# A decoder trunk on one core: split weights kept in DRAM, the place ahead of the MLP reordered, and the convolution tied behind the wide block's queries

## The chip, the cores and the metric

The kernel runs on one core of a Trainium2 chip. The metric is the device time of one execution in microseconds; a kernel's time is the median of several runs. TensorE (PE) does the matrix products, VectorE (DVE) and ScalarE (ACT) the elementwise work, GpSimd (POOL) a little of it, and SyncE (SP) issues nearly all DMAs.

## The reference

One layer over 1024 rows of width 1024, all in float32. `mix` stands for the recurrent parts in the middle:

```python
h = rms_norm(x, norm_mix)
xa, ga, q, f, v, g, m_a, m_b = split(h @ w_in)          # eight projections of 1024
xa = causal_depthwise_conv(xa, conv_w, conv_b)          # four taps
y_a = rg_lru(xa, w_r, w_i, lam) * gelu(ga)              # gated linear recurrence
o = hgrn2_chunkwise(silu(q), (1-lb)*sigmoid(-f), log(f_gate), v)
y_b = rms_norm(o, hg_norm) * silu(g)
x = x + (sigmoid(m_a) * y_a + sigmoid(m_b) * y_b) @ w_out
h = rms_norm(x, norm_mlp)
x = x + square(relu(h @ w_up)) @ w_down
return rms_norm(x, norm_final)
```

## The kernel before, in words

**Products.** Every float32 product is made of three matmuls (`mm3`, L130): each operand is split into a high part, rounded to the fast float32 form by ScalarE (`split`, L87), and the rest, which VectorE subtracts (L88); then high x high, high x low and low x high are summed in PSUM. A weight tile of 128 x 1024 is thus loaded raw (`load_w`, L95, 512 KB), cast on ScalarE and subtracted on VectorE before PE can use it.

**Stages in time.** The mixer works on two halves of 512 rows (c = 0, 1) and four pairs of heads (p), which makes eight stages i = 4c + p. Stage i+1's projections on PE are interleaved with the recurrent block `hgrn` of stage i: `go(n)` in `hgrn` runs n steps of the next stage. The weights of a pair are used twice, once in each half, and are loaded and split both times. After the mixer come the gate products (16 "quads", seven products each by a Strassen-like plan, `PLAN`), the output projection, the second norm with its transposes, the MLP's up products (16 quads, the same plan) and the down products.

**Weight order.** `seq` lists the weight tiles in the order of use: 72 projection tiles (36 different ones), four tiles of gate weights used at the end of the mixer, then three rounds of eight output tiles: one for rows 0 to 511 (`out_proj`), and one for each of the two "parts" (256 rows each) of the second half. `next_w` hands out the next tile, and `fill_w` loads and splits ahead of it. Raw tiles have four buffers, split tiles six (three pairs of high and low).

**Order of work.** A planner puts every engine's instructions in order by priority (place in the program, raised by `high_priority`) and by its own estimate of when each is ready; each engine, SP's queue of DMAs too, then works strictly in that order. Where `pinned` is set PE keeps the order of the program. It is set in the mixer from the end of stage 0's first projection on.

**Around the change.** In `hgrn`, three blocks of small products are made per stage (L513), then VectorE works out `kc`, `qb`, `kk` and last `qf` (L598 to L612, the helper's line is L503), and PE multiplies `qf` by `kk` in the wide block (L642). `pk` (L668) transposes `kk` after one more multiply on VectorE. The next stage's convolution (`conv`, L405, three passes on each of two tiles, L411) is emitted during the q projection; its split result `xcH`, `xcL` is read by the products `pr` and `pi` of `rg_lru`. In the second half GpSimd also makes operand combinations for the gates (`make_combos`, L303).

Ahead of the MLP the residual rows go out to `x2d` (L871), come back as `x2a` (L1150), are normed (`norm_rows`, L151), transposed on PE (L1161) and split into the operands B11, B21, B22, B12. From these `combos` makes t1, n2, T3, T4 (L893 to L896). The rows of the second half come straight from the output projection's second half (L1190). `quad_steps` turns the raw tiles of a quad into its weights: "a" is A11, "sums" and then "b" and "c" give s1 to s4, "d" gives A12 and A22.

Of the kernel before, what the change touches and what calls it, by code (L numbers as in the profile page):

```python
# [44 lines left out]
def trunk(ctx: ExitStack, tc: tile.TileContext, x, wts, mlp, pv, gains, mask_f, mask_u, out):  # L45
# [28 lines left out]
    for c in range(NC + 1):  # L74
        seq += [wts[MIX_TILES + j] for j in range(OUT_TILES)]
    most = [n_mix]
    ready, made = {}, [0]
# [11 lines left out]

    def raw_tile(name):  # L90
        return wp.tile([P, 1024], F32, tag="raw", name=name, bufs=4)
# [5 lines left out]

    def split_w(i, raw):
        h = wp.tile([P, 1024], F32R, tag="w", name=f"wH{i}", bufs=6)
        lo = wp.tile([P, 1024], F32R, tag="w", name=f"wL{i}", bufs=6)  # L100
        with tc.high_priority(400):
            split(raw, h, lo)
        return h, lo
# [3 lines left out]
    def fill_w(n):  # L107
        while made[0] < min(n, most[0]):
            i = made[0]
            raw = raws.pop(0) if raws else load_w(i)  # L110
            ready[made[0]] = split_w(i, raw)
            made[0] += 1

    def get_w(i, ahead=2):
        fill_w(i + ahead + 1)
        return ready.pop(i)
# [288 lines left out]
    def conv(c, p, xc, xps):  # L405
        for s in range(2):
# [3 lines left out]
            for j in range(3):  # L410
                V.scalar_tensor_tensor(  # L411
# [6 lines left out]
                )  # L418
            if c + 1 < NC:
                G.tensor_copy(xcar[:, u, :], xp[:, T : T + 3])  # L420
# [78 lines left out]
    def hgrn(c, p, got, go):  # L499
# [112 lines left out]
        mul(pairs(qf)[:, :, 1, :], q8[:, :, 1, :], t8[:, :, 0:1].to_broadcast([P, 16, 32]))  # L612
# [146 lines left out]
    def stage(i):  # L759
# [19 lines left out]
        def convolve():  # L779
            got["xc"] = conv(c, p, xc, xps)  # L780
# [124 lines left out]
    def quad_steps(i, pools, raws=raw_tile, minus=False):  # L905
# [22 lines left out]
        def pair(src, names):  # L928
            def go():
                h, lo = (pools[1].tile([P, 1024], F32R, tag="w", name=f"w{names[0]}{i}{q}", bufs=6) for q in "HL")  # L930
# [128 lines left out]
    def ykt(c, ku):  # L1059
        p, s = divmod(ku, 2)  # L1060
        t = yt[c][p]
        s = s if c == 0 else 1 - s
        return t[:, 0, s, :], t[:, 1, s, :]

# [7 lines left out]
    for q in own[:2]:  # L1072
        load_quad(GQ + q, dma=in_turn if q == own[0] else load_late)
        gwork[q] = quad_steps(GQ + q, (w1p, wp), minus=True)
        with tc.high_priority(600):
            gwork[q]["a"]()
            if q == own[0]:
                gwork[q]["sums"]()
                gwork[q]["d"]()
    for o in ("t1", "n2"):  # L1080
        load_combo(o)
    in_turn(raw_q[GQ + own[1]][1], mlp[GQ + own[1], 1])
    for o in ("T3", "T4"):
        load_combo(o)
# [4 lines left out]
    gwork[own[0]]["b"]()  # L1089
# [4 lines left out]
    for q in own:  # L1094
# [3 lines left out]
        for step in (1, 2, 4, 5, 6) if q == own[0] else (0, 1, 2, 3, 4, 5, 6):  # L1098
# [4 lines left out]
            if q == own[0] and step == 2:  # L1103
# [14 lines left out]
            for k in {2: ("sums", "a", "b"), 5: ("c",), 6: ("d",)}.get(step, ()):  # L1118
                if q > own[0] or k != "a":
                    gwork[n][k]()  # L1120
        gate_work(q)
# [3 lines left out]
    close_hB()  # L1125
    y1p, close_y = opened("y1p")
    y_tiles(y1p, 1)
# [7 lines left out]
    n2p, close_n2 = opened("n2")  # L1135
# [329 lines left out]
```

## Time and profile before

| | |
|---|---|
| median of 3 runs | 1588.41 us (1586.48 to 1588.73) |
| profiled execution, its own time | 1585.07 us |
| its span, first to last instruction | 1583.3 us |
| busy: PE / DVE / ACT / POOL | 1531.4 / 1209.5 / 820.8 / 162.6 us |
| granted clock of TensorE, mean | 0.992 |
| DMA moved | 280.07 MB, mean 177 GB/s |

The span in 40 equal slices, each digit the busy share in tenths:

```profile
PE   7989999999999999999999978999999999999998
...
DVE  5797586696876938686856488988778888888877
ACT  5656756557475534454533376777677632211113
POOL 1021110234436600000000000000000000000000
```

A slice is 39.6 us. The mixer ends in the fifteenth, the gates run to the middle of the twenty-third, the place ahead of the MLP is the twenty-fourth and twenty-fifth (PE 7 and 8), up products follow to the thirty-second and the down products to the end. In the views a row of the timeline is: start, duration, engine, line, operation, output <- inputs, shapes, count, and in brackets the idle time before it with what ended it. A row of the windows view is: window, its length, then busy time and (x) instructions for PE, PE's weight loads, DVE, ACT and POOL, then the granted clock, the DMA share and GB/s.

### The profile page before, as it was taken

To read this page: it belongs to the slowest core of one execution; us is meant where nothing else is said; L and a number is where in the kernel's file an instruction comes from. 1 tells how busy PE (TensorE), PEld (TensorE's weight loads), DVE (VectorE), ACT (ScalarE), POOL (GpSimd) and SP (SyncE) were. 2 spreads that over 40 slices of the span, in tenths; PEclk is the share of its full clock that TensorE was granted. 3 is DMA by queue.
4 is the path that set the end of the run, shared out by engine and by line. 5 is a ranking of instruction groups with operands and counts; after the bars stand their busy time and mean duration, and the time that the engine had idled before them with its cause. 6 is when DMAs were issued, how large, how long until landed. Compare 5 with 4: busy or idle time off the path is not lost.

```text
span 1583.3 us, 23131 instructions
## 1 busy us (share of the span) xinstructions
PE 1531.4 (97%) x9072; PEld 1278.8 (81%) x9072; DVE 1209.5 (76%) x1706; ACT 820.8 (52%) x1341; POOL 162.6 (10%) x187
## 2 busy tenths in 40 slices
PE   7989999999999999999999978999999999999998
PEld 6878888888788888888888767888888878888886
DVE  5797586696876938686856488988778888888877
ACT  5656756557475534454533376777677632211113
POOL 1021110234436600000000000000000000000000
PEclk9999999999999999999999999999999999999999
DMA  6223122232343375332328762766666675666652
GB/s 241 96 94 107 67 103 85 94 121 94 134 137 118 106 269 199 130 117 96 134 95 310 260 212 80 279 253 252 253 249 248 226 273 226 246 255 254 254 199 107
DMA packets 72205, 280.07 MB, mean 177 GB/s; under 512 B 7712, under 2 KB 16032, under 8 KB 59168
## 3 DMA queue, kind: packets, MB, share of 16 engines
q1 hardware_dynamic: 69072, 267.58, 45.3%
q10 hardware_dynamic: 3024, 11.01, 1.9%
q8 instruction: 71, 1.16, 0.3%
q14 instruction: 38, 0.31, 0.1%
HBM read 193.63 MB, written 84.93 MB: 176 GB/s over the span
## 4 chain that ended last, share of the span: by engine, by line
PE 76%; DVE 13%; ACT 6%; issue 2%; DMA 2%; POOL 1%; DVEq 0%; SPq 0%; POOLq 0%; ACTq 0%
PE dX L132 3%; PE dX L133 3%; PE uX L132 3%; PE dX L134 3%; PE uX L134 3%; PE gX L134 3%; PE gX L133 3%; PE uX L133 3%; PE gX L132 3%; PE uY L134 2%; PE gY L134 2%; PE gY L133 2%; PE uY L132 2%; PE uY L133 2%; PE gY L132 2%
## 5 line engine op out<-in xcount | busy, mean ns | idle before, releaser
L88 DVE TENSOR_TENSOR wL<-raw,wH 128x1024 fp32r<-128x1024 f32 x100 | 124.3, 1245 | 91.4 <-ACT wH L87 89.9
L87 ACT CAST wH<-raw 128x1024 fp32r<-128x1024 f32 x100 | 105.0, 1050 | 71.2 <-PE po L133 36.6
L1374 DVE TENSOR_TENSOR acc<-acc,dX 128x512 f32<-128x512 f32 x128 | 85.1, 685 | 29.3 <-PE dX L134 28.7
L87 ACT CAST wA<-q 128x512 fp32r<-128x512 f32 x46 | 28.4, 621 | 132.6 <-PE dX L134 101.4
L1374 DVE TENSOR_TENSOR acc<-acc,dY 128x512 f32<-128x512 f32 x64 | 43.5, 686 | 15.7 <-PE dY L134 14.5
L133 PE MATMUL po<-wL,y 128*128 128x512 f32 x128 | 50.0, 391 | 0.0
L134 PE MATMUL po<-wH,y 128*128 128x512 f32 x128 | 50.0, 391 | 0.0
L132 PE MATMUL po<-wH,y 128*128 128x512 f32 x128 | 49.8, 389 | 0.0
L1234 ACT ACTIVATE b<-b 128x512 f32<-128x512 f32 x48 | 30.2, 632 | 35.7 <-DVE b L1233 35.7
L155 POOL TENSOR_TENSOR rstd_h<-rstd_h,mhalf 128x1 f32<-128x1 f32 x8 | 5.5, 687 | 385.1 <-DVE rstd_h L154 385.1
L411 DVE SCALAR_TENSOR_TENSOR xc<-xp,pvt,xc 128x512 f32<-128x512 f32 x48 | 40.4, 864 | 0.0
L710 ACT ACTIVATE on<-po 128x128 f32<-128x128 f32 x64 | 16.9, 278 | 44.9 <-PE po L706 44.9
L88 DVE TENSOR_TENSOR wA<-q,wA 128x512 fp32r<-128x512 f32 x46 | 31.5, 686 | 10.3 <-ACT wA L87 10.3
L324 POOL TENSOR_TENSOR stt<-r,stt 128x256 fp32r<-128x256 f32 x16 | 23.2, 1467 | 93.1 <-ACT stt L323 93.1
L915 DVE TENSOR_TENSOR s<-q,q 128x512 f32<-128x512 f32 x46 | 31.6, 688 | 1.2 <-DMA q<-mlp_in 0.7
L920 DVE TENSOR_TENSOR s<-q 128x512 f32<-128x512 f32 x46 | 31.6, 687 | 0.4
L1235 ACT ACTIVATE b<-b 128x512 f32<-128x512 f32 x48 | 30.1, 631 | 1.1
L132 PEld LDWEIGHTS po<-wH,y 128*128 128x128 f32 x128 | 24.0, 188 | 5.0
L134 PEld LDWEIGHTS po<-wH,y 128*128 128x128 f32 x128 | 24.0, 188 | 4.9
L133 PEld LDWEIGHTS po<-wL,y 128*128 128x128 f32 x128 | 24.0, 188 | 4.9
L703 PE MATMUL po<-v,scT 128*128 128x128 f32 x128 | 24.7, 286 | 2.8 <-DVE sn L689 2.8
L616 POOL TENSOR_SCALAR scT<-dd 32x256 f32<-32x256 f32 x32 | 22.0, 687 | 50.4 <-DVE dd L532 48.9
(2528 smaller groups left out, 5422.6 us busy)
## 6 DMA issues: line engine op xcount, KB each, us to landing
raw<-wts_in SPq DMA_DIRECT2D x96, 512.0 KB, 3.4
q<-mlp_in SPq DMA_DIRECT2D x92, 512.0 KB, 3.5
y<-yd SPq DMA_DIRECT2D x7, 1024.0 KB, 8.7
x<-x_in SPq DMA_DIRECT2D x8, 512.0 KB, 6.0
hd<-ri SPq DMA_DIRECT2D x16, 256.0 KB, 2.7
od<-onT ACTq DMA_DIRECT2D x8, 512.0 KB, 4.4
cdT<-stT SPq DMA_DIRECT2D x16, 256.0 KB, 3.3
o<-od SPq DMA_DIRECT2D x4, 1024.0 KB, 7.3
```

Of the source, the lines that this page charges most:

```text
L87: keep(A.copy(h, src))
L88: keep(V.tensor_tensor(out=lo, in0=src, in1=h.bitcast(F32), op=ALU.subtract))
L132: pin(PE.matmul(o, ah, bh, start=first, stop=False, **how))
L133: pin(PE.matmul(o, ah, bl, start=False, stop=False, **how))
L134: pin(PE.matmul(o, al, bh, start=False, stop=last, **how))
L411: V.scalar_tensor_tensor(xc[:, s, :], xp[:, j : j + T], pvt[:, PV_CW + 8 * j + u : PV_CW + 8 * j + u + 1], xc[:, s, :], op0=ALU.mult, op1= ...
L703: pin(PE.matmul(on_ps, scT[:, 4 * s + n, :], vn(s, n), start=True, stop=only))
L915: V.tensor_tensor(out=sa[:, 0, :], in0=a21, in1=a22, op=ALU.add)
L920: V.tensor_tensor(out=sb[:, 0, :], in0=a21, in1=a11, op=ALU.add)
L1234: A.activation(b[:, at, :], b[:, at, :], AF.Relu, scale=-1.0 if at == 2 else 1.0)
L1235: A.activation(b[:, at, :], b[:, at, :], AF.Square)
L1374: V.tensor_tensor(out=dst, in0=dst, in1=banks[bk, pr], op=op)
```

## The change

Three edits, with what they need of each other:

- **Weights.** The high and low part of a weight are now one tile of [128, 2, 1024] (three buffers, as many bytes as before), and raw tiles are halves of such tiles (two buffers, each freed when both halves are read). When a projection tile is split for the first of its two uses, the split pair is stored to DRAM (1 MB); for the second use it is loaded as it is, in turn into "w" and "raw" buffers, up to five ahead, and isn't split. Four of the output tiles stay in SBUF for both parts, so 20 are loaded instead of 24.
- **Convolution.** From stage 2 on each of its passes is ordered on VectorE behind the multiply that writes the second half of `qf` in the block before (L612). It is an order within the engine's queue, without a semaphore.
- **Ahead of the MLP.** The pools for the norm and for the single weights are opened before the first output projection; y is loaded in two parts; part 1 takes the two column halves in the other order, and its last tiles one row block after the other; the first up products with B11 go between the last transposes; t1, n2, T3 and T4 of all row blocks are made after that, one operand at a time (`rest_of_it`); quad 0's steps run as 0, 3, 1, 2, 5, 4, 6. In the gates the first quad's loads, b, and steps 4 and 5 change places.

The diff's core:

```diff
+    for j in [*range(OUT_TILES), *range(OUT_TILES), *range(OUT_TILES // 2)]:
+        seq += [wts[MIX_TILES + j]]
+    to_raw = n_mix + 2 * OUT_TILES - 1
...
     def raw_tile(name):
-        return wp.tile([P, 1024], F32, tag="raw", name=name, bufs=4)
+        if spare:
+            return spare.pop()
+        t = wp.tile([P, 2, 1024], F32, tag="raw", name=name, bufs=2)
+        spare.append(t[:, 1])
+        return t[:, 0]
...
+            k = pair_tiles[i] if i < len(pair_tiles) else None
+            if k in wd:
+                t = w_tile(f"wC{i}", ("w", "raw")[cached[0] % 5 % 2])
+                cached[0] += 1
+                with tc.high_priority(400):
+                    nc.sync.dma_start(t.bitcast(F32), wd[k])
+            else:
+                raw = raws.pop(0) if raws else load_w(i)
+                t = split_w(i, raw)
+                if k is not None and k in pair_tiles[i + 1 :]:
+                    wd[k] = dram.tile([P, 2, 1024], F32, tag=f"wd{k}", name=f"wd{k}")
+                    nc.sync.dma_start(wd[k], t.bitcast(F32))
+            ready[i] = (t[:, 0], t[:, 1])
...
-    def get_w(i, ahead=2):
-        fill_w(i + ahead + 1)
+    def get_w(i):
+        fill_w(i + (5 if cached[0] else 3))
...
+                if behind is not None:        # in conv, after each pass
+                    how = mybir.DependencyInfo(mybir.DependencyClass.NoSync, mybir.DependencyReason.DATA)
+                    tc.add_manual_dep(ins.ins, behind.ins.name, how, reason="behind")
...
-        mul(pairs(qf)[:, :, 1, :], q8[:, :, 1, :], t8[:, :, 0:1].to_broadcast([P, 16, 32]))
+        got["wide"] = mul(pairs(qf)[:, :, 1, :], q8[:, :, 1, :], t8[:, :, 0:1].to_broadcast([P, 16, 32]))
...
-            got["xc"] = conv(c, p, xc, xps)
+            got["xc"] = conv(c, p, xc, xps, gots[i - 1]["wide"] if i > 1 else None)
...
                 gwork[q]["sums"]()
+                gwork[q]["b"]()
                 gwork[q]["d"]()
-    for o in ("t1", "n2"):
-        load_combo(o)
+                for o in ("t1", "n2", "T3"):
+                    load_combo(o)
     in_turn(raw_q[GQ + own[1]][1], mlp[GQ + own[1], 1])
-    for o in ("T3", "T4"):
-        load_combo(o)
+    load_combo("T4")
...
-        for step in (1, 2, 4, 5, 6) if q == own[0] else (0, 1, 2, 3, 4, 5, 6):
+        for step in (1, 2, 5, 4, 6) if q == own[0] else (0, 1, 2, 3, 4, 5, 6):
...
-            if q == own[0] and step == 2:
+            if q == own[0] and step == 4:
                 gate_step(own[1], 0)
...
+        late = half == 0 and tt > 1           # in second_norm
...
+            xs = n2p.tile([P, D], F32, tag=f"y0{2 * tt - 4}" if late else "x2a", name=f"x2a{t}")
...
+        home = {2: "y01", 3: "y03", 5: "x2a", 6: "y00", 7: "y02"}.get(t, "xn")
+        xn = n2p.tile([P, D], F32, tag=home, name=f"xn_h{t}", bufs=3 if home == "xn" else 1)
...
+    def first_weights():
+        for q in (0, 1):
+            load_quad(q)
+            work[q] = quad_steps(q, (w1p, wp))
+            work[q]["a"]()
+            if q == 0:
+                work[0]["sums"]()
+                work[0]["b"]()
...
-        for hf in range(2):
+        for hf in (part, 1 - part):
             pp = {tt: bank("pj", f"po1{hf}{tt}") for tt in tts}
-            for j in range(4):
-                wh, wl = next_w()
+            turn = [(j, tts) for j in range(4)]
+            if (part, hf) == (1, 0):
+                turn = turn[:2] + [(j, tts[i : i + 1]) for i in range(2) for j in (2, 3)]
+                pinned[0] = True
+            w = w_two if (part, hf) == (1, 1) else {}
+            if (part, hf) == (0, 1):
+                w_two = w
+            for n, (j, those) in enumerate(turn):
+                if j not in w:
+                    w[j] = next_w()
+                if n == 4:
+                    first_weights()
...
-        for tt in tts:
+        for i, tt in enumerate(tts):
+            if part:
+                product(i, 0)
             nc.sync.dma_start(x2d[4 + tt], x2s[tt])
-            second_norm(tt, 1)
+            rest.append(second_norm(tt, 1))
+    rest_of_it()
...
+    with tc.high_priority(400):
+        work[0]["d"]()
+        work[0]["c"]()
+    for q, step in ((0, 0), (1, 0), (0, 3), (0, 1), (0, 2), (0, 5), (0, 4), (0, 6)):
+        with tc.high_priority(300):
+            hidden(q, step)
+        if (q, step) == (0, 2):
+            work[1]["sums"]()
+    pinned[0] = False
+    work[1]["b"]()
+    work[1]["c"]()
+    work[1]["d"]()
```

143 lines of the change are left out of this document (79 added, 64 removed).

## The prediction

> **What bounds the kernel now.** I read the page first, then PE's own waits, then windows around each wait (idle time and granted clock), then the timelines of VectorE and TensorE in one stage of the second half, and last the transfers.
>
> ```profile
> span 1583.3 us, 23131 instructions
> PE 1531.4 (97%) x9072; PEld 1278.8 (81%) x9072; DVE 1209.5 (76%) x1706; ACT 820.8 (52%) x1341; POOL 162.6 (10%) x187
> ...
> PE xT_h L1161 <- DVE rstd_h L154: 6.3, 1, 6.3
> PE sc L642 <- DVE qf L503: 4.7, 3, 1.6
> PE xT_h L1161 <- DVE xn_h L156: 4.1, 4, 1.8
> ...
> PE sc L631 <- DVE qb L503: 1.5, 3, 0.5
> PE sc L642 <- ACT scT L647: 1.4, 1, 1.4
> ```
>
> TensorE is busy 97% of the span, and the change removes no matmul. So it can win only PE's idle time, 1583.3 - 1531.4 = 51.9 us, and time in which PE runs at a lower clock. The waits name two places that the change touches: the wide block `sc` behind `qf` and `qb` on VectorE (mixer, 6.2 us in three pairs), and the transposes `xT_h` (before the MLP, 10.4 us). The windows show what these cost.
>
> ```profile
> core 0: us, PE busy (x) PEld busy (x) DVE busy (x) ACT busy (x) POOL busy (x), PEclk, DMA share, GB/s
> 352.00:355.00 3.00, 0.94 (x35) 0.75 (x34) 3.00 (x5) 1.57 (x2) 2.84 (x3) 1.00 0.00 0
> ...
> 482.00:485.00 3.00, 0.96 (x35) 0.68 (x34) 3.00 (x5) 1.57 (x2) 2.77 (x4) 1.00 0.00 0
> 485.00:489.00 4.00, 4.00 (x22) 3.50 (x23) 4.00 (x6) 2.96 (x5) 1.46 (x2) 0.57 0.09 19
> ...
> 580.00:880.00 300.00, 300.00 (x1327) 248.46 (x1326) 210.39 (x221) 133.88 (x175) 0.00 (x0) 1.00 0.45 165
> ...
> 906.00:928.00 22.00, 18.00 (x93) 14.20 (x92) 17.23 (x23) 16.88 (x28) 2.70 (x4) 1.00 0.85 300
> 942.00:956.00 14.00, 6.88 (x31) 5.33 (x30) 12.37 (x20) 9.07 (x19) 2.25 (x3) 0.64 0.45 166
> 956.00:978.00 22.00, 18.51 (x83) 14.06 (x81) 18.81 (x29) 14.13 (x24) 0.00 (x0) 1.00 0.11 38
> ...
> 950.00:956.00 6.00, 5.37 (x20) 4.45 (x21) 4.85 (x9) 4.66 (x10) 1.40 (x2) 0.50 0.37 126
> ```
>
> Each of the three mixer waits (the first and, with what follows it, the last are shown) idles PE 2.06 us, and then the clock falls to a mean of 0.57 over 4 us, which loses 4 x 0.43 = 1.7 us of matmul work more: 3.8 us a time, 11.3 us for three. Ahead of the MLP PE idles 4.0 + 7.1 + 3.5 = 14.6 us, and 5.4 us of its work at clock 0.50 lose 2.7: 17.3 us. The gates (580 to 880) have no idle PE: there the rearranged loads can only lose. A 512-column matmul has a pitch of 300 / 1327 = 0.226 us.
>
> [...]
>
> **The mixer's second half.** In its four last stages 36 weight tiles are loaded already split, and the convolution of the stage being projected comes behind `qf` of the block before it.
>
> ```profile
> 401.59 1.27 DVE L88 TENSOR_TENSOR wL<-raw,wH 128x1024 fp32r<-128x1024 f32 x1
> ...
> 407.18 1.23 DVE L88 TENSOR_TENSOR wL<-raw,wH 128x1024 fp32r<-128x1024 f32 x1
> ...
> 409.71 3.28 DVE L411 SCALAR_TENSOR_TENSOR xc<-xp,pvt,xc 128x512 f32<-128x512 f32 x3
> ...
> 413.21 0.93 DVE L411 SCALAR_TENSOR_TENSOR xc<-xp,pvt,xc 128x512 f32<-128x512 f32 x1
> ...
> 414.25 1.29 DVE L503 TENSOR_TENSOR kc<-kc,seg 128x768 f32<-128x768 f32 x1
> 415.46 2.11 DVE L503 TENSOR_TENSOR qb<-qb,seg 128x256 f32<-128x256 f32 x2
> 417.50 1.21 DVE L503 TENSOR_TENSOR kk<-kc,seg 128x512 f32<-128x512 f32 x1
> 418.64 1.21 DVE L503 TENSOR_TENSOR qf<-qb,seg 128x512 f32<-128x512 f32 x1
> ...
> 424.43 0.69 DVE L503 TENSOR_TENSOR kk<-kk,seg 128x512 f32<-128x512 f32 x1
> ...
> 409.29 0.88 PE L513 MATMUL sc<-qb,kc 128*32 128x48 f32 x64
> ...
> 419.99 1.81 PE L642 MATMUL sc<-qf,kk 128*64 128x64 f32 x16 [1.57 <-DVE qf L503]
> ...
> 229.73 1.15 PE L642 MATMUL sc<-qf,kk 128*64 128x64 f32 x16
> ...
> 233.66 1.03 PE L668 MATMUL pk<-ident,kk 128*128 128x128 f32 x8
> ...
> 436.53 0.39 PE L132 MATMUL pr<-xcH,wH 128*128 128x512 f32 x1
> ...
> 420.51 1.06 POOL L316 TENSOR_TENSOR r<-r 128x256 f32<-128x256 f32 x1
> ...
> 220.13 2.05 DVE L411 SCALAR_TENSOR_TENSOR xc<-xp,pvt,xc 128x512 f32<-128x512 f32 x3
> ```
>
> This is one such stage; the rows at 220 to 234 are one of the first half. VectorE is full here (3.00 of 3.00 in the first window above). The chain kc, qb, kk, qf takes 419.8 - 414.25 = 5.5 us and starts late because two splits (2.5 us) and 4.2 us of convolution stand ahead of it since 401.6. Without them it is held only by PE, which reads `kc` until 410.2; qf is then done at 410.2 + 5.5 = 415.7. PE reaches L642 five projection steps (5 x 6 x 0.226 = 6.8 us) and the small block L631 after 410.2 (0.7 us, an estimate: L642 itself has 1.15 where nothing holds it), at 417.7. The 2.06 us go, with 2 us to spare, and the clock's 1.7 us with them.
>
> What is late next: six convolution passes now follow at 415.7. By the shown mean of the first three, 3.28 / 3 = 1.1 us, they take 6.6; by 0.93 each, 5.6. So VectorE comes to the second `kk` multiply (424.43 now) at 421.3 to 422.3, plus about 1 us of masked copies (an estimate from the rest of this stretch). The transposes `pk` wait for that multiply. In the first half they come 233.66 - 229.73 = 3.9 us after L642, so here at 417.7 + 3.9 = 421.6. The new wait is 421.3 + 0.7 - 421.6 = 0.4 up to 422.3 + 1 + 0.7 - 421.6 = 2.4 us, nothing if the planner puts the multiply between passes. I take 0.8, near the low end: the passes take 0.68 us in the first half (2.05 / 3), where GpSimd is idle, and GpSimd's last combination here starts at 420.51. The other reader of the convolution, `pr`, starts at 436.5 and has over 10 us. So 3 x (3.8 - 0.8) = 8.9 us won (bounds 3 x (3.8 - 2.4) = 4 and 11.3). The fourth wait (1.4 us on `scT`) stands behind the split of a gate tile, which is still split: nothing.
>
> ```profile
> L88 DVE TENSOR_TENSOR wL<-raw,wH 128x1024 fp32r<-128x1024 f32 x100 | 124.3, 1245 | 91.4 <-ACT wH L87 89.9
> L87 ACT CAST wH<-raw 128x1024 fp32r<-128x1024 f32 x100 | 105.0, 1050 | 71.2 <-PE po L133 36.6
> ...
> raw<-wts_in SPq DMA_DIRECT2D x96, 512.0 KB, 3.4
> ...
> y<-yd SPq DMA_DIRECT2D x7, 1024.0 KB, 8.7
> ...
> SPq L95 <- DVE wL L88: 202.4, 51, 17.3
> ```
>
> The splits themselves: 36 + 4 of 100 go, 40 x 1.245 = 50 us of VectorE and 40 x 1.05 = 42 us of ScalarE. Nearly all lies beside PE and is worth nothing except in the chain above and ahead of the MLP. The loads double in size; one of 1 MB lands in 8.7 us at worst by the row for `y`, and five buffers of 24 x 0.226 = 5.4 us each give it over 20. No cost.
>
> **The mixer's first half.** 36 stores of 1 MB join SP's queue. A store waits there for its split, and what is queued behind it (the next raw load, `hd`, later `cd`) waits too. SP already stands up to 17.3 us at a load for a free raw buffer, so loads run ahead of the splits, and a store becomes ready just when the next raw pair does. I take nothing; the bound is the third rival. The convolution's new place can open the `pk` wait in three stages here: 0.2 us each, 0.5 in all, by the 0.68 us passes.
>
> **Gates.** Raw buffers come in pairs, so a load waits for two readers. T3 and b are brought forward and steps 4 and 5 change places: an arrangement against that. PE has no idle there, cost 0 to 3, I take 0.
>
> **Ahead of the MLP.** Four splits fall away, the last product of each row block runs on while the norm of the one before is worked out, two products with B11 go between the last transposes, and the combinations t1, n2, T3, T4 of all blocks go to the end, one operand at a time.
>
> ```profile
> 901.54 4.41 DMA x2a<-x
> ...
> 909.33 5.32 DMA x2a<-x
> ...
> 909.32 1.09 PE L1161 MATMUL xT_h<-ident,xn_h 128*128 128x128 f32 x8 [1.40 <-DVE xn_h L156]
> ```
>
> The first 4.0 us (906 to 928) stay: the rows of x2 go out and come back (4.41 us), and the second block's load still waits for the first one's buffer (5.32 us). The middle 7.1 us and the 2.7 us of clock should go: after the last matmul of block 2 PE still has 12 matmuls of block 3 and 12 of the first product, 24 x 0.226 = 5.4 us, against a norm of 3.4 us (from the landing at 901.54 + 4.41 = 905.95 to the transposes at 909.32). But quad 1's load needs the raw pair that quad 0 holds until its `d` split, and `d` needs a weight pair that PE frees only after block 2's end T, by six matmuls of block 3 (1.4 us). 1.4 + split 2.3 + load 3.4 + a split of half the size 1.2 gives T + 8.3; PE wants it after the rest of block 3, the first product and a set of transposes, at T + 2.7 + 2.7 + 1.1 = T + 6.5. A wait of some 2 us is new. Of the last 3.5 us (the first seven products wait for operands) I leave 2. Sum: 17.3 - 4.0 - 2 - 2 - 0.4 for odd gaps = 8.9 us won. Bounds: 0 (the new wait grows to 6 us and brings the clock loss back) to 13.
>
> **The sum.** 8.9 - 0.5 + 8.9 = 17.3 us. The profiled execution took 1585.1 us (its span and 1.8 us around it); it becomes 1567.8. The median of the timed runs stands 3.3 us above that execution, so the forecast is 1571 us.
>
> **The rivals.**
> First, the front gains nothing: the queue pair - split - weight buffer - load takes the place of the wait removed. For it: six raw and weight users share two and three pairs. Against it: VectorE has less to do there. 1571 + 8.9 = 1580 us.
> Second, the convolution only moves the stall: if `pk` waits long enough at 2.4 us to drop the clock (1.7 more), the second half keeps none of its 11.3 us and pays 3 x 0.3; three first-half stages may pay 2 each. 1571 + 8.9 + 0.9 + 5.5 = 1586, no change.
> Third, slower: the stores pace the first half. If SP's order is load, store, load, store, a load goes out only when the split before it is done, and one tile takes 2.3 (split) + landing, against PE's 5.4. It decides from a landing of 3.1 us; the median is 3.4 already, and the stores add traffic. At 4.0 us it is 0.9 x 36 = 32 us: 1603 us. Against it speaks that SP's waits are for raw buffers, two tiles ahead of the split.
> That VectorE isn't relieved at all cannot be: the casts and subtractions aren't issued, and the tie is an order within one engine.
>
> **How the numbers follow.** Chances: forecast 0.55, first rival 0.18, second 0.12, third 0.15. A difference of 0.2% (3.2 us) is about what a measurement of this kernel can tell from none. Faster: 0.55 + 0.18 + 0.02 (of the second) = 0.75; same 0.07; slower 0.15 + 0.03 = 0.18. The range starts at 1558, where all of it is won, what I let stay too (11.3 + 17.3 + 1.4 = 30 us below the median of 1588.4), and reaches 1590, past the first two rivals; the third is left out.
>
> **What would show it.** Right: L88 and L87 with 60 tiles instead of 100; no wait of PE at L642 behind qf in the second half, and clock 1.00 after it; a wait at L668 below 1.5 us; PE's idle time between the end of the first output projection and the eighth product down from 14.6 to 8 to 9 us, without a stretch at 0.50. Wrong: PE waiting in the first half for `wH` or `wL` behind a load, L668 waiting over 2 us with half clock behind it, or a wait for `wA` of quad 1 of over 4 us.

## Result, and the profile after

The changed kernel is slower, by 0.6%: 1596.43 us (median of four runs, 1595.14 to 1601.16) against 1587.45 for the kernel before in the same runs, a ratio of 1.0064 with an interval of 1.0047 to 1.008. The forecast was 1571, in a range of 1558 to 1590. The head, two of the groups and two of the transfers on the page of after:

```profile
span 1599.4 us, 22994 instructions
PE 1539.1 (96%) x9072; PEld 1283.7 (80%) x9072; DVE 1164.6 (73%) x1666; ACT 777.8 (49%) x1301; POOL 150.4 (9%) x187
...
L89 DVE TENSOR_TENSOR wS<-raw,wS 128x1024 fp32r<-128x1024 f32 x60 | 74.1, 1238 | 52.8 <-ACT wS L88 52.7
...
L88 ACT CAST wS<-raw 128x1024 fp32r<-128x1024 f32 x60 | 62.8, 1049 | 67.4 <-PE po L154 30.8
...
wd<-wS SPq DMA_DIRECT2D x36, 1024.0 KB, 4.8
wC<-wd SPq DMA_DIRECT2D x36, 1024.0 KB, 5.4
```

The 40 splits are gone and VectorE has 45 us less to do, as planned. But PE has no less idle time (1599.4 - 1539.1 = 60.3 us instead of 51.9), and the same 9072 matmuls take 7.7 us longer. PE's waits (total, times, longest) say where:

```profile
PE pkv L701 <- ACT kT L696: 4.8, 6, 1.4
PE xT_h L1202 <- DVE rstd_h L174: 4.3, 3, 3.5
PE sc L536 <- issue: 4.1, 2, 2.6
PE po L152 <- DVE xs L885: 3.1, 1, 3.1
PE pk L691 <- DVE kk L526: 2.9, 3, 1.5
...
PE g L152 <- ACT v L393: 2.0, 1, 2.0
...
PE sc L665 <- DVE qf L526: 0.5, 1, 0.5
```

The wait of the wide block behind `qf` (4.7 us before) and the 6.3 us wait of the transposes are gone or smaller. In their place stand five that the kernel before has smaller or not at all: `pkv` behind ScalarE's `kT`, small products for which nothing but "issue" is named, the residual addition `xs`, `pk`, and `g` behind `v`.

The profiled execution of after was the longest of its four (1601.16 us); a repeat of the same kernel (`k1_again`) has a profile at its median, and the tables use that one. Sections are cut in PE's timeline at the first `gX`, the first `po`, the last `uX` with B11 and the end of the last matmul; a stage runs from one `pk` to the next, so stage 7 is the last of the mixer:

| us | mixer | gates | output projection to up | rest |
|---|---|---|---|---|
| before | 580.1 | 266.6 | 403.6 | 325.1 |
| after, again | 590.7 | 268.8 | 398.5 | 328.1 |
| no tie | 584.4 | 268.8 | 398.7 | 329.5 |
| pairs of buffers alone | 588.4 | 274.5 | 416.8 | 329.7 |
| no tie, casts earlier | 576.0 | 268.5 | 398.9 | 329.2 |
| no tie, three ahead | 585.0 | 268.2 | 393.0 | 329.8 |
| all three mends | 576.1 | 268.6 | 393.3 | 329.0 |
| single buffers, loads, casts earlier | 578.8 | 266.7 | 406.7 | 324.2 |

| stage, us | 1 | 2 | 3 | 4 | 5 | 6 | 7 |
|---|---|---|---|---|---|---|---|
| before | 61.6 | 66.7 | 61.4 | 65.3 | 65.0 | 65.0 | 62.8 |
| after, again | 64.8 | 67.3 | 65.8 | 62.0 | 63.5 | 63.4 | 71.4 |
| no tie | 62.8 | 67.0 | 64.9 | 62.4 | 62.2 | 62.9 | 69.8 |
| tie alone | 60.7 | 67.2 | 62.0 | 65.0 | 65.2 | 65.0 | 67.9 |
| pairs alone | 60.7 | 66.9 | 61.7 | 66.9 | 67.4 | 67.8 | 63.9 |
| no tie, casts earlier | 63.5 | 67.0 | 63.5 | 62.4 | 62.2 | 61.8 | 62.9 |

Against before the repeat loses 8.2 us in stages 1 to 3, wins 6.4 in stages 4 to 6, loses 8.6 in stage 7, 2.2 in the gates and 3.0 at the end, and wins 5.1 ahead of the up products: 10.5 us worse. By the medians it is 7.7. The one profile of the kernel before (1585.07 us) lies some 3.4 us under the median of its runs, so every comparison of sections with it overstates a loss by about as much; stage 7 is where that shows (below).

### The profile page after: what moved, and what is told of

Read it like the earlier page. It is cut to its first block, busy times and chain, and to the rows that moved or that the text cites. A ratio compares the mean times of both kernels' runs of the same rounds, so it can differ in the third digit from the quotient of the medians.

```text
span 1599.4 us, 22994 instructions
## 1 busy us (share of the span) xinstructions
PE 1539.1 (96%) x9072; PEld 1283.7 (80%) x9072; DVE 1164.6 (73%) x1666; ACT 777.8 (49%) x1301; POOL 150.4 (9%) x187
## 3 DMA queue, kind: packets, MB, share of 16 engines
q8 instruction: 71, 1.16, 0.3%
## 4 chain that ended last, share of the span: by engine, by line
PE 72%; DVE 15%; ACT 7%; issue 3%; DMA 3%; POOL 0%; SPq 0%; DVEq 0%; ACTq 0%; POOLq 0%
PE dX L152 3%; PE dX L153 3%; PE dX L154 3%; PE uX L153 3%; PE uX L154 3%; PE uX L152 3%; PE gX L152 2%; PE gX L154 2%; PE gX L153 2%; PE dY L152 2%; PE dY L153 2%; PE dY L154 2%; PE pj_xa L152 2%; PE pj_xa L153 2%; PE pj_xa L154 2%
## 5 line engine op out<-in xcount | busy, mean ns | idle before, releaser
L88 ACT CAST ws<-s 128x1024 fp32r<-128x1024 f32 x92 | 96.7, 1052 | 141.0 <-PE dY L154 38.1
L88 ACT CAST wA<-q 128x512 fp32r<-128x512 f32 (+1 forms) x92 | 76.7, 835 | 135.4 <-PE dX L154 61.0
L89 DVE TENSOR_TENSOR wA<-q,wA 128x512 fp32r<-128x512 f32 (+1 forms) x92 | 87.2, 954 | 48.0 <-ACT wA L88 45.9
L89 DVE TENSOR_TENSOR ws<-s,ws 128x1024 fp32r<-128x1024 f32 x92 | 112.2, 1221 | 13.1 <-ACT ws L88 13.1
L89 DVE TENSOR_TENSOR wS<-raw,wS 128x1024 fp32r<-128x1024 f32 x60 | 74.1, 1238 | 52.8 <-ACT wS L88 52.7
L88 ACT CAST wS<-raw 128x1024 fp32r<-128x1024 f32 x60 | 62.8, 1049 | 67.4 <-PE po L154 30.8
L152 PE MATMUL po<-wS,y 128*128 128x512 f32 x128 | 51.1, 400 | 3.1 <-DVE xs L885 3.1
L153 PE MATMUL po<-wS,y 128*128 128x512 f32 x128 | 51.1, 399 | 0.0
L154 PE MATMUL po<-wS,y 128*128 128x512 f32 x128 | 51.0, 398 | 0.0
L1318 ACT COPY e<-uX 128x512 f32<-128x512 f32 x32 | 18.7, 584 | 27.9 <-PE uX L154 27.9
L478 DVE TENSOR_TENSOR ri<-ri,xc 128x1024 f32<-128x1024 f32 x8 | 9.8, 1223 | 30.3 <-ACT ri L457 30.3
L152 PEld LDWEIGHTS po<-wS,y 128*128 128x128 f32 x128 | 24.7, 193 | 8.6 <-issue 3.5
L153 PEld LDWEIGHTS po<-wS,y 128*128 128x128 f32 x128 | 24.8, 193 | 5.0
L154 PEld LDWEIGHTS po<-wS,y 128*128 128x128 f32 x128 | 24.6, 193 | 5.2
```

The costliest lines, as they stand in the source:

```text
L88: keep(A.copy(h, src))
L89: keep(V.tensor_tensor(out=lo, in0=src, in1=h.bitcast(F32), op=ALU.subtract))
L152: pin(PE.matmul(o, ah, bh, start=first, stop=False, **how))
L153: pin(PE.matmul(o, ah, bl, start=False, stop=False, **how))
L154: pin(PE.matmul(o, al, bh, start=False, stop=last, **how))
L1318: A.copy(e_of[q, step], o)
```

## Experiments

Ratios are to the kernel before, run on the same chip in turn, with their 95% interval.

**Part by part.** The unchanged kernel again (`k1_again`):

> The changed kernel once more, to set beside the three below. The trace so far: the mixer ends 12.6 us later than before (580.1 to 592.7), in two pieces: stages 2 to 4 lose 9.7 us, the four of the second half win 6.1, the last stage loses 8.6. Both theories expect 1594 to 1598 us and the same places; a stall of TensorE marked issue that is a chance of one execution would not come back at the same blocks (158, 291, 421 us).

1595.9 us, 1.0048 (1.0028 to 1.0068). Without the tie (`k1_no_tie`):

```diff
-            got["xc"] = conv(c, p, xc, xps, gots[i - 1]["wide"] if i > 1 else None)
+            got["xc"] = conv(c, p, xc, xps, None)
```

> Without the tie: the convolution's passes may again stand ahead of kc, qb, kk and qf. Theory A (the stored weights' DMAs starve TensorE of instructions and the last stage's GpSimd work is moved onto the chain): the tie is worth about 4 us per stage of the second half, so this is 4 to 10 us slower than the changed kernel, 1600 to 1606. Theory B (the tie itself costs, by pk and pkv waiting behind the passes): 3 to 8 us faster than the changed kernel, 1588 to 1593.

1589.48 us, 1.0009 (0.9999 to 1.0018): beside stores and loads the tie costs 6.4 us. Without stores and loads (`k1_no_cache`), and with the stores but no loads (`k1_stores_only`):

```diff
-            if k in wd:
+            if k in wd and False:                                   # both
-                if k is not None and k in pair_tiles[i + 1 :]:
+                if False:                                           # k1_no_cache alone
-        fill_w(i + (5 if cached[0] else 3))
+        fill_w(i + (5 if i >= len(pair_tiles) else 3))              # both
```

> Without stored weights: both halves load raw and split, the tie and the place ahead of the MLP as changed. Theory A: the issue stalls at 158, 291 and 421 us go, the first half is back to the periods of before (61.6, 66.7, 61.4 us instead of 64.5, 68.9, 66.0) and the last stage too (62.8 instead of 71.4); the time is 1580 to 1586, below the kernel before. Theory B: no better than the changed kernel, 1594 or more, since VectorE has 36 splits more.

> The 36 stores stay, but the second use is split again as before, so this is the kernel without stored weights plus 36 stores that nobody reads. Theory A: the issue stalls of the first half that fall beside a store (158 us) stay, those beside a load (291 and 421 us) go; the stores alone cost 2 to 6 us against the kernel without stored weights. Theory B: the stores cost nothing, under 1 us.

1593.49 us (1.0041, 1.0027 to 1.0055) and 1593.35 (1.0039, 1.0025 to 1.0053): where nothing is loaded back, the stores cost nothing that can be measured. Without both the stalls marked issue are gone and stages 1 to 3 are within 1.1 us of before (61.2, 67.4, 62.2), as theory A had it, but the time falls by only 2.4 us, to between the two theories. Neither cache nor tie (`k2_front_only`: the two edits above together), and the tie alone in the kernel before (`k2_tie_only`: the `behind` edit of the change and nothing else):

> Paired buffers and the place ahead of the MLP as changed, without stored weights and without the tie: all that is left of the change behind the mixer. From the three kernels run so far gates to up products are 3.0 us shorter than before and the rest 3 to 4.5 us longer. Theory C (what the front wins is lost again where the up products give way to the down products, and the paired buffers cost the mixer nothing): 1587 to 1590 us, no change. Theory D (paired buffers cost the mixer too): 1591 or more.

> The kernel before and the tie, nothing else. Theory B (the tie moves the wait from L642 to the transposes pk, which then wait 2.8 us in the second half, as in the kernel without stored weights): the waits at L642 are gone and pk waits 2.6 to 3.0 us three times; 1589 to 1593 us. My prediction's reckoning (0.8 us at pk in place of 3.8 us): 1578 to 1581.

1594.8 us (1.0047, 1.0029 to 1.0066) and 1591.99 (1.0032, 1.0017 to 1.0046). So without the cache the tie costs nothing (1593.49 with it, 1594.8 without), and alone in the kernel before 3.0 us. In `k2_tie_only`, where weights are still split, VectorE's and PE's timelines show what the tie does to a stage of the second half:

```profile
351.91 0.96 DVE L411 SCALAR_TENSOR_TENSOR xc<-xp,pvt,xc 128x512 f32<-128x512 f32 x1
352.79 1.75 DVE L88 TENSOR_TENSOR wL<-raw,wH 128x1024 fp32r<-128x1024 f32 x1
...
357.83 1.53 DVE L411 SCALAR_TENSOR_TENSOR xc<-xp,pvt,xc 128x512 f32<-128x512 f32 x2
359.29 0.88 DVE L506 TENSOR_TENSOR kk<-kk,seg 128x512 f32<-128x512 f32 x1
...
360.22 0.88 PE L671 MATMUL pk<-ident,kk 128*128 128x128 f32 x6 [2.88 <-DVE kk L506]
```

The convolution, with a weight split among it, now stands ahead of the second `kk` multiply, and `pk` waits 2.88 us where the wide block waited 2.06. The stages keep their 65 us: the stall has moved, which was the second rival.

The mixer of after with the old order behind it (`k2_mixer_only`: everything from the gates on as before, but with paired buffers), and the loads with one store (`k2_loads_only`: every second use reads back the same stored tile in place of its own, which leaves out 35 of the 36 stores):

```diff
-    for j in [*range(OUT_TILES), *range(OUT_TILES), *range(OUT_TILES // 2)]:      # k2_mixer_only
+    for j in [*range(OUT_TILES), *range(OUT_TILES), *range(OUT_TILES)]:
...
-                    wd[k] = dram.tile([P, 2, 1024], F32, tag=f"wd{k}", name=f"wd{k}")      # k2_loads_only
-                    nc.sync.dma_start(wd[k], t.bitcast(F32))
+                    if not wd:
+                        wd[k] = dram.tile([P, 2, 1024], F32, tag=f"wd{k}", name=f"wd{k}")
+                        nc.sync.dma_start(wd[k], t.bitcast(F32))
+                    else:
+                        wd[k] = list(wd.values())[0]
```

> Stored weights and the tie, with gates, front and MLP in the order of before (paired buffers kept). Theory C: the mixer ends 10.6 us late as in the changed kernel, and all behind it as before: 1597 to 1600 us, slower than the changed kernel. Theory E (the losses behind the mixer come from the paired buffers, not from the new order): the rest after the up products still is 3 us longer, 1600 or more.

> One split tile is stored and is loaded again for every second use, in place of the tile that belongs there: this leaves out 35 of the 36 stores and keeps all 36 loads. Theory A (stores and loads each hold up TensorE's instructions where they meet the blocks of small products): the stall at 158 us goes, the one at 290 us stays, 1592 to 1595 us. If the stores alone were to blame, the stall at 290 us would go as well.

1621.03 us (1.0215, 1.0193 to 1.0236) and 1592.37 (1.0032, 1.0017 to 1.0046). In the second the stall near 158 us is gone and the one near 286 us stays. It is 3.5 us under `k1_again`, so beside loads the stores may cost something; the two intervals overlap. The first was far above the 1597 to 1600 us of theory C, and theory E blames the pairs, so the pairs of buffers were put into the kernel before by themselves (`k3_pairs`: `raw_tile`, `split_w` and `pair` of the change, no cache, no tie, the old order):

```diff
-        return wp.tile([P, 1024], F32, tag="raw", name=name, bufs=4)
+        t = wp.tile([P, 2, 1024], F32, tag="raw", name=name, bufs=2)
...
-        h = wp.tile([P, 1024], F32R, tag="w", name=f"wH{i}", bufs=6)
-        lo = wp.tile([P, 1024], F32R, tag="w", name=f"wL{i}", bufs=6)
+        t = w_tile(f"wS{i}", "raw" if i == to_raw else "w")
```

> The kernel before with nothing changed but the buffers: two pairs of raw tiles and three pairs of split tiles in place of four and six single ones; no stores, no loads, no tie, the order in front of the MLP as before. Theory A (pairs alone cost the mixer its time): the mixer ends at about 586 to 587 us instead of 580, with the waits of sc on qb and on scT in the second half (3.5 us instead of 2.06), and the part behind the gates is 10 to 17 us longer, as in the kernel with the mixer of after alone (417.8 instead of 403.6): 1600 to 1612 in all. Theory B (the new order in front of the MLP, or something else of that version, moved the mixer): it ends at 580 to 581 and the time is 1587 to 1592.

1619.67 us, 1.0201 (1.0183 to 1.0219), above both theories: 31 us for buffers of the same bytes in larger pieces. They cost every section, 8.3, 7.9, 13.2 and 4.6 us. The changed order, with four output tiles kept, wins 5.7 and 18.3 us of that back in the gates and behind them (268.8 and 398.5 against 274.5 and 416.8). In the mixer's second half, VectorE and PE of `k3_pairs`:

```profile
345.56 4.42 DVE L431 SCALAR_TENSOR_TENSOR xc<-xp,pvt,xc 128x512 f32<-128x512 f32 x4
...
350.20 0.93 DVE L431 SCALAR_TENSOR_TENSOR xc<-xp,pvt,xc 128x512 f32<-128x512 f32 x1
351.05 1.50 DVE L526 TENSOR_TENSOR kc<-kc,seg 128x768 f32<-128x768 f32 x1
...
354.70 0.70 PE L654 MATMUL sc<-qb,kc 128*32 128x32 f32 x32 [1.92 <-DVE qb L526]
356.97 1.97 PE L665 MATMUL sc<-qf,kk 128*64 128x64 f32 x16 [1.57 <-ACT scT L670]
```

All six convolution passes, not five, now precede `kc`, and the waits are 3.49 us instead of 2.06. That the planner orders them so because a weight's buffer comes free at another moment fits these rows; no run isolates it.

**The last stage.** In the kernels with loads whose casts stand where they stood it takes 69.7 to 71.4 us, against 62.8 in the profile of before. GpSimd and VectorE of after in it:

```profile
518.75 2.95 POOL L344 TENSOR_TENSOR stt<-r,stt 128x256 fp32r<-128x256 f32 x2 [10.92 <-ACT stt L343]
...
531.41 1.06 POOL L336 TENSOR_TENSOR r<-r 128x256 f32<-128x256 f32 x1
...
526.68 1.31 DVE L526 TENSOR_TENSOR q<-q,f 128x512 f32<-128x512 f32 x1
527.88 1.19 DVE L526 TENSOR_TENSOR kb<-kk,f 128x512 f32<-128x512 f32 x1
529.00 1.76 DVE L526 TENSOR_TENSOR qa<-q,f 128x1024 f32<-128x1024 f32 x1
```

GpSimd waits 10.92 us for a cast that ScalarE has put behind the block's sigmoids, and then works through VectorE's chain, whose products take 0.4 to 0.5 us longer than in the kernel before (0.88, 0.71 and 1.25 us there). `k3_cast_first` (no tie) calls the casts one step earlier in that stage:

```diff
+        if i == 7:
+            combos_on(1)
         fs = hooked(project_steps(c, f"f{c}{p}"), {6: convolve} if i == 1 else {})
...
-            combos_on(1 if i == 4 else 2)
+            combos_on(1 if i in (4, 7) else 2)
```

> No tie; in the last stage of the mixer the casts of a combination piece on ScalarE are issued ahead of the f projection, so ahead of the four sigmoids of the gates' block, behind which they stood (they began at 509.9 us in the kernel without the tie, at 501.1 us in the kernel before), and GpSimd's 13 us of work on the piece start some 20 us sooner. Theory A (the last stage is 7 to 8.6 us longer because GpSimd works beside VectorE's chain at 515 to 525 us, where VectorE's operations take 1.3 to 3 times as long): the stage falls from 69.8 to 62 to 65 us, the VectorE scan products of that stretch go back to their lengths of before, and the time from 1589.5 to about 1583, below the kernel before. Theory B (the loaded weight tiles, not GpSimd, lengthen the stage): it stays at 69 to 71 us and the time at 1588 to 1591.

1583.36 us, 0.9973 (0.9962 to 0.9984), stage 7 62.9 us. The piece is done at 501.8, and the same three products have their short times back:

```profile
501.06 0.74 POOL L336 TENSOR_TENSOR r<-r 128x256 f32<-128x256 f32 x1
...
514.71 0.88 DVE L526 TENSOR_TENSOR q<-q,f 128x512 f32<-128x512 f32 x1
515.50 0.69 DVE L526 TENSOR_TENSOR kb<-kk,f 128x512 f32<-128x512 f32 x1
516.10 1.23 DVE L526 TENSOR_TENSOR qa<-q,f 128x1024 f32<-128x1024 f32 x1
```

The 62.8 us of before are themselves partly luck. GpSimd and VectorE there:

```profile
527.60 9.65 POOL L324 TENSOR_TENSOR stt<-r,stt 128x256 fp32r<-128x256 f32 x2 [13.57 <-ACT stt L323]
...
529.55 0.72 DVE L915 TENSOR_TENSOR s<-q,q 128x512 f32<-128x512 f32 x1
```

The same in `k3_plain_stores` (below), which has the same order of instructions there on VectorE, ScalarE and GpSimd, and whose median is that of the kernel before:

```profile
529.39 3.81 POOL L329 TENSOR_TENSOR stt<-r,stt 128x256 fp32r<-128x256 f32 x2 [13.54 <-ACT stt L328]
...
531.42 1.18 DVE L920 TENSOR_TENSOR s<-q,q 128x512 f32<-128x512 f32 x1
```

In before the first of GpSimd's two products takes 8.04 us and VectorE keeps its pace (0.72 us in the row above). In `k3_plain_stores` that product takes 2.67 us, nine VectorE operations in a row take 0.43 to 0.51 us more, and the stage takes 67.6 us; in `k2_tie_only` it is 2.67 and 67.9. So up to 4.8 of the 8.6 us can be a chance of the one profile of before. The 6.1 us of the earlier casts are a difference of medians and don't rest on it.

**The output projection.** PE's new wait there and VectorE beside it, in the timeline of the kernel without the tie:

```profile
876.33 1.23 DVE L89 TENSOR_TENSOR wS<-raw,wS 128x1024 fp32r<-128x1024 f32 x1 [2.48 <-ACT wS L88]
877.47 1.28 DVE L885 TENSOR_TENSOR xs<-po,xs 128x512 f32<-128x512 f32 x2
...
878.30 0.77 PE L152 MATMUL po<-wS,y 128*128 128x512 f32 x1 [3.09 <-DVE xs L885]
```

The window behind it (PE, its weight loads, DVE, ACT, POOL, clock, DMA share, GB/s):

```profile
878.30:882.00 3.70, 3.70 (x9) 2.96 (x10) 0.45 (x1) 0.00 (x0) 0.00 (x0) 0.54 0.94 249
```

The addition that frees PE's bank is queued behind a split whose buffer came free only when PE was done. `k3_ahead3` (no tie) splits five ahead only as far as the mixer's tiles:

```diff
-        fill_w(i + (5 if cached[0] else 3))
+        fill_w(i + (5 if cached[0] and i < n_mix else 3))
```

> No tie; weight tiles are split five ahead only in the mixer and three ahead in the output projection, as in the kernel before. Theory A (the new wait of 3.08 us of po on the residual addition is there because a split of a tile five ahead, for which no buffer is free yet, stands ahead of the addition on VectorE): the wait and the half clock behind it go, output projection to up falls by about 4 us from 398.7, and the time from 1589.5 to about 1585. Theory B (the addition waits for the transfer of the residual, which the 4 MB of y loads delay): the wait stays, and the time within 1 us of 1589.5.

1584.58 us, 0.9975 (0.9964 to 0.9985); the wait is gone, the addition comes first, and PE is busy through at full clock (872 to 876 us, clock 1.00). VectorE there:

```profile
873.14 0.69 DVE L885 TENSOR_TENSOR xs<-po,xs 128x512 f32<-128x512 f32 x1 [4.45 <-PE po L154]
873.75 1.22 DVE L89 TENSOR_TENSOR wS<-raw,wS 128x1024 fp32r<-128x1024 f32 x1
```

**The stores alone.** `k3_plain_stores` is the kernel before with single buffers; each split is also stored, as two transfers of 512 KB:

```diff
+            h, lo = ready[made[0]] = split_w(i, raw)
...
+                for n, t in enumerate((h, lo)):
+                    nc.sync.dma_start(wd[:, n, :], t.bitcast(F32))
```

> The kernel before, which with single buffers also stores each of the 35 split tiles that are used twice, as two transfers of 512 KB; nothing is loaded back. Theory A (dense transfers hold up TensorE's instructions in the blocks of small products): one or two waits marked issue of 1.3 to 1.9 us appear among the small products of the first half (near 150 to 165 us), the first stages grow by 2 to 4 us, and the time is 1589 to 1593. Theory B (those waits come with the pairs of buffers or the tie): none appears, and the time is 1587 to 1589, as before.

1588.11 us, 1.0003 (0.9991 to 1.0014): the stall of theory A, the time of theory B. A price cannot be told from none, though stage 1 of its profile is 1.7 us longer. Of its PE timeline:

```profile
156.97 0.37 PE L518 MATMUL sc<-qb,kc 128*32 128x48 f32 x13 [1.64 <-issue]
```

The window ahead of it:

```profile
150.00:156.00 6.00, 5.33 (x192) 4.26 (x192) 4.89 (x9) 2.92 (x5) 0.38 (x2) 1.00 1.02 393
```

**All together.** `k4_both` has no tie and both mends; `k4_tie_fixed` both mends with the tie; `k4_singles` is the kernel before with stores and loads in single buffers, the loads running five ahead, and the earlier casts, without pairs, tie or new order:

```diff
+            if k in wd:                                                # k4_singles, in fill_w
+                tag, bufs = (("w", 6), ("raw", 4))[cached[0] % 5 % 2]
...
+                t = [wp.tile([P, 1024], F32R, tag=tag, name=f"wC{q}{i}", bufs=bufs) for q in "HL"]
+                with tc.high_priority(400):
+                    for n in range(2):
+                        nc.sync.dma_start(t[n].bitcast(F32), wd[k][:, n, :])
```

> No tie, the casts of the combination piece ahead of the f projection in the last stage, and splits five ahead only in the mixer: the three mends together. Theory A (three separate losses in three places): the gains of 6.1 and 4.9 us from 1589.5 add up, so 1578 to 1579, 10 us below the kernel before; last stage 63 us, output projection to up 393. Theory B (the waits that go are replaced by one another's successors): 1582 to 1585, no better than one mend alone.

> The changed kernel with its tie kept, and with the other two mends (casts ahead of the f projection in the last stage, splits five ahead only in the mixer). Theory A (the tie has a cost of its own, by the waits of pkv on kT of 1.4 us and of pk in each stage of the second half, and by a later convolution): 6 us above the kernel with all three mends, 1584 to 1586, with the three stages of the second half at 62.0, 63.5 and 63.5 us. Theory B (the tie cost only because it made the last stage worse): within 2 us of that kernel, 1578 to 1581.

> The kernel before with the stored and loaded weights alone, in its single buffers (two transfers of 512 KB for a tile), five ahead in the second half, and the casts ahead of the f projection in the last stage; no pairs of buffers, no tie, the order in front of the MLP as before. Theory A (pairs and the new order cancel each other, and only the loaded weights win): the mixer ends near 574 to 576 us, gates 266.6, output projection to up 403.6, rest 325, so 1577 to 1581, within 2 us of the kernel with all three mends. Theory B (the new order in front of the MLP is worth what the prediction gave it): 1584 or more, 6 us behind that kernel.

`k4_both` takes 1578.53 us, 0.994 (0.992 to 0.996), 10 us less than the kernel before and 18 less than the change as given: the three losses add up. `k4_tie_fixed` takes 1585.74 (0.9986, 0.9973 to 0.9999), 7.2 us more, so beside stores and loads the tie has a cost of its own (by the stages 1.6 in 1 to 3, 2.8 in 4 to 6, 2.8 in 7). `k4_singles` takes 1583.53 (0.9976, 0.9963 to 0.9988), between its two theories: once mended, pairs and new order together are worth 5 us. By the sections they win 13.4 us behind the gates and 2.7 in the mixer, and give back 1.9 in the gates and 4.8 at the end, 9.4 in all; the profile of `k4_singles` lies 2.5 us over its median and that of `k4_both` 1.2 under.

## Why the prediction was wrong

The forecast was 17.3 us won; by the medians 7.7 to 9 were lost. The steps that failed are four: the tied convolution's reader, taken to have over 10 us; "nothing" for the last stage; "I take nothing" for the stores and "no cost" for the loads; and a look-ahead of five, which was priced for loads and also governs splits. What the runs showed in place of each follows, in the order of the sum.

**The second half: mechanism right, credited to the wrong part.** The three waits at L642 did go, and with them the clock loss. But the loads, in their paired buffers, do it alone: without the tie stages 4 to 6 take 62.4, 62.2 and 62.9 us, 7.8 less than before; with it the win is 6.4. Without it the wait that is left is short and the clock stays up (`k4_both`):

```profile
358.59 1.12 PE L665 MATMUL sc<-qf,kk 128*64 128x64 f32 x16 [1.32 <-DVE qf L526]
```

The window around it:

```profile
358.00:362.00 4.00, 3.41 (x26) 3.00 (x27) 3.94 (x7) 2.28 (x4) 2.22 (x3) 1.00 0.01 4
```

The step that failed is "What is late next". The `pk` wait came out as forecast (0.73 and 0.63 us in two of three stages, 0.8 taken). What was not followed is ScalarE: the reader of the convolution was taken to be `pr`, ten microseconds away, but between them lies the cast `xcH`. ScalarE and PE of after:

```profile
366.40 1.05 ACT L88 CAST xcH<-xc 128x1024 fp32r<-128x1024 f32 x1 [3.13 <-DVE xc L431]
...
369.37 1.08 ACT L503 ACTIVATE sq<-pj_q 128x512 f32<-128x512 f32 x2
370.34 0.87 ACT L696 COPY kT<-pk 128x384 f32<-128x384 f32 x2
...
370.88 1.60 PE L701 MATMUL pkv<-v,kT 128*128 128x128 f32 x12 [1.38 <-ACT kT L696]
```

The tied convolution ends at 366.3, ScalarE idles 3.13 us for it, and everything queued behind that cast is late, `kT` last, for which PE waits 1.0 to 1.4 us more in each stage.

The clock loss that the prediction counts three times was one observation and not three. In the traces of before and after the clock falls to 0.50 for 3.41 us or a multiple of it (3.41, 6.83 or 10.24, but for the last stretch, which the end of the kernel cuts), and within each of the two all such stretches begin at whole multiples of 3.413 us from each other. The three stretches of before begin at 355.29, 420.14 and 485.00 us, 64.85 us apart, which is 19 of these steps: the same wait fell three times at the same place of a step.

**The last stage ("The fourth wait ... nothing"): 8.6 us, of which 6.1 are shown.** The prediction checked the wait it could see and not what the shifted order does to GpSimd's pieces. The earlier casts alone take 6.1 us off (1589.48 to 1583.36).

**The first half: a loss of 0.5 was one of 8.2.** Without the tie it is still 5.0. The tie's share is 3.2 us by these stages and 1.6 by the two `k4` kernels; four kernels without the tie differ by up to 2.4 there. Alone in the kernel before it costs 0.2 there, no more than forecast. Most of the rest goes with a wait that no row of the kernel before shows, "issue" among the small products beside dense transfers; in the timeline of after:

```profile
291.79 0.44 PE L536 MATMUL sc<-qb,kc 128*32 128x48 f32 x11 [2.60 <-issue]
```

The windows before, around and behind it:

```profile
285.00:289.00 4.00, 4.00 (x129) 3.23 (x129) 1.11 (x3) 0.80 (x2) 0.00 (x0) 1.00 0.96 339
289.00:292.00 3.00, 0.40 (x27) 0.26 (x15) 0.69 (x3) 0.00 (x0) 0.00 (x0) 0.99 0.09 27
292.00:295.00 3.00, 3.00 (x17) 2.31 (x9) 2.66 (x5) 1.24 (x2) 0.00 (x0) 0.50 0.03 8
```

Such a wait, of 1.36 to 1.91 us, stands at 156 to 159 us in all eleven profiles with stores of every tile, one of 1.85 to 2.60 us at 285 to 292 in all ten with loads, and neither in any other. In all 21 places PE stops behind the same product of its block, the 51st of 64 near 158 us and the 53rd near 290 (in after these are the 2231st and the 4523rd matmul or weight load). The trace shows one thing more beside them. The pages of before and after list "q8 instruction: 71, 1.16", that is 71 packets of 16 KB, for 18,144 matmuls and weight loads. In after PE goes on 1.26 and 1.47 us after the 8th and the 17th of these packets have ended (at 157.19 and 290.32 us). The same two begin at the 1983rd and the 4273rd matmul or weight load in before, where there is no stall, and at the 2138th and the 4523rd in after. So beside the dense transfers of after they came 155 and 250 instructions later; that PE waits for them is inferred from this order, and no run isolates it. "No cost" for loads held for their landing (5.4 us by the page of after) but not for what they do to others. The third rival (loads paced by stores) did not come: PE has no wait for a weight in the first half, and without loads the time is the same with stores and without them.

**Gates: "Raw buffers come in pairs ... I take 0".** The 2.2 us are within the stated 0 to 3, because of the new order: pairs alone cost 31 us over the kernel (`k3_pairs`), 7.9 of it in the gates. The prediction priced the pairs in the gates and for quad 1's load; they also work in the mixer and in the step from up to down, and most of the rearrangement only pays for them (`k2_front_only`, pairs with the new order, takes 1594.8 us, 25 less than pairs alone).

**Ahead of the MLP: the idle time was right by luck, its parts were not.** PE's waits at `xT_h` and `uX` in after are 1.37 + 0.92 + 0.56 + 3.48 + 0.65 = 7.0 us, with the smallest ones 7.7, against a forecast of 8 to 9 from 14.6. The wait of 2 us for quad 1's weights did not appear, and of the last 3.5 us 1.2 are left. But of the middle 7.1 us, which should go, one wait of 3.48 is left, and half clock behind it, the opposite of one of the signs named for being right. The window of after:

```profile
971.00:975.00 4.00, 4.00 (x16) 3.44 (x15) 3.40 (x6) 1.89 (x4) 0.73 (x1) 0.57 0.65 253
```

The step behind it is "a norm of 3.4 us" against 5.4 us of products. The norm of that block takes 5.9 us (from 964.91 on ScalarE to the transposes at 970.82), because two splits and an addition stand ahead of `rstd_h` on VectorE from 965.34 to 968.21. Further, the split of a tile five ahead put a wait of 3.1 us into the output projection, with half clock behind it (0.54; 4.9 us by `k3_ahead3`), an edit that the prediction priced only for the mixer. And 3.0 us are lost at the end, for which the sum has no term. Pairs alone already cost 4.6 there.

In sum, three of these losses are shown by removing them (tie, late casts, five ahead: 18 us, 1596.4 to 1578.5). With them mended (`k4_both`) both wins of the forecast are there, 9.2 us in stages 4 to 6 and 10.3 ahead of the up products, and what is lost is 4.6 in stages 1 to 3 (3.8 of it the two stalls), 2.0 in the gates and 3.9 at the end. What the pairs cost in each section is shown as a whole, not by its mechanism. The stalls marked issue are shown to come and go with the dense transfers; their price in time could not be told from zero for the stores.

## What to carry to other kernels

When work is taken off a full engine, follow every queue that its results feed, to the end of the stage: the wait removed here came back on ScalarE (a cast behind the delayed convolution) and on GpSimd (work that slid beside VectorE's chain). Buffers of the same bytes in larger pieces were not free (31 us here). A look-ahead chosen for loads was wrong for splits, because a split queued ahead for a buffer that was not free held up the addition behind it, and PE 3.09 us with it. And a profile is one execution: before a section's loss is explained, the profile that it is measured against is set beside its kernel's median (here 3.4 us apart), and waits that recur at equal distances are counted as one observation.

## What the runs showed of the hardware

- **Transfers and TensorE's pauses.** Behind stretches of 4 to 6 us with a DMA share of 0.96 to 1.02 (339 and 393 GB/s, 129 and 192 small matmuls in the windows above) PE paused 1.4 to 2.6 us with nothing but "issue" named. Two transfers of 512 KB did it (1.64 us in `k3_plain_stores`, 1.36 and 2.49 in `k4_singles`) as one of 1 MB did (1.46 and 2.60 us in after). In after PE went on 1.26 and 1.47 us after the 8th and the 17th packet of the queue "q8 instruction" had ended, and these two began 155 and 250 matmuls and weight loads later than in before.
- **VectorE beside GpSimd.** VectorE's operations of 128 to 1024 columns took about the same 0.4 to 0.5 us longer, whatever their length, where GpSimd got on (in after against before 0.86 instead of 0.36 us at 128 columns, 1.76 instead of 1.25 at 1024); where one GpSimd product of 256 columns took 8.04 us instead of 0.7 (before) VectorE kept its pace. Both came with the same order of instructions (before and `k3_plain_stores`).
- **The clock.** Half clock followed waits of 3.09 us (0.54), 2.60 us (0.50) and 0.49 + 1.57 us with 0.7 us of small products between (0.57), but not one of 1.32 us, nor in `k2_tie_only` one of 2.88 us at `pk`, where the next windows show 1.00. So the length of a wait alone did not tell. The traces of before and after, each cut into steps of 3.413 us in line with its own stretches of half clock, have 879 steps at full clock from 25 us to 1560 us. The 11 with 1.89 us or more of idle PE were all followed by half clock, of the three with 1.68 to 1.77 us one was, and of the other 865 (1.55 us or less) none. The three waits of before left 2.04 to 2.09 us in one step each.
